# Fifteen-product matmul with tanh gating: four plain row tiles and twenty triples, w loaded by column pieces, seven x tiles transposed on TensorE, x sums on VectorE

## The chip, the core and the metric

The kernel runs on one core of one Trainium2 chip. The metric is the device time of one execution in microseconds. A core has five engines that run side by side and meet at semaphores: TensorE (PE in the profile, with PEld for its weight loads) multiplies and transposes, VectorE (DVE) and ScalarE (ACT) do elementwise work and can read PSUM, GpSimd (POOL) does elementwise work on SBUF and issues the DMA transfers that cast, and SyncE (SP) issues plain DMA transfers and DMA transposes. Each engine works through its own queue in order: an instruction that waits holds back everything queued behind it on that engine. PSUM, where matmul results land, has eight banks of 128 x 512 f32 here.

## The reference

x has 16 x 512 rows of 1024 numbers, w1 and w2 are 1024 x 768, all f32:

```python
y1 = np.matmul(x, w1)
y2 = np.matmul(x, w2)
return (np.tanh(y1) * y2).astype(np.float32)
```

## The kernel before

**Row tiles and pieces.** The rows of x are 64 tiles of 128. Multiplying wants x with its inner dimension across the partitions, so each tile is transposed into `xT`, eight blocks of 128 x 128 in f16. w1 and w2 stand side by side in f16 in `wh`. The 768 columns of each weight are cut into F = 512 and G = 256; the two G parts together are again 512 wide, so there are three column blocks ("a" of w1, "b" of w2, "M" for the two G parts), and with the inner dimension in two halves six weight blocks. A plain row tile needs 3 x 8 = 24 matmuls of 512 columns.

**Triples.** Three row tiles with six halves, times the six weight blocks, can be done with 15 products of sums of blocks instead of 18: `A_SUMS` lists ten sums of x halves for each triple (L385, `x_sum`), `B_SUMS` eleven sums of weight blocks made once (L375, `w_sum`), and `C_OPS` the 15 products p0 to p14 of four matmuls each (L426, `product`) with the additions (L441, `c_add`), copies and seeds (L432, `c_copy`), tanh (L444, `c_tanh`) and multiplies (L449, `c_mul`) that put them together in PSUM and SBUF. A triple costs 60 matmuls where three plain tiles cost 72. A number such as 32 or 24 names a block or a sum of blocks by its bits.

**What is plain.** The first `HEAD = 6` tiles and the last `TAIL = 1` are plain (L399 `mm`, L405 tanh, L409 multiply); 19 triples lie between. The last tile's three groups of matmuls are put into gaps near the end, behind the places `FILL = (-10, -6, -4)` of the product order.

**How x gets in.** Tiles 0 to 3 are loaded as f32 by SP (L307), transposed on TensorE into PSUM (L324) and copied to `xT` in f16 by VectorE or ScalarE. All other tiles are loaded by GpSimd with a cast to f16 into one of six `xh` buffers (L334) and transposed by a DMA that SP issues (L338) into `xT`, for which there are four buffers for each of three tags. GpSimd's first load stands behind a small copy, `gate`, that waits for the third slice of w2 (L470). The weights come as 16 slices of 128 x 768, four of them on ScalarE's queue (L311), and are cast to f16 by VectorE, ScalarE or, for w2, GpSimd (L317, L315).

**Side work.** ScalarE sums the absolute values of every x tile and weight slice (L341). At the end one flag says whether all of them were in a range where f16 serves; a general path stands behind a branch for the case that they weren't.

**What sets the order.** Everything is pinned in program order, and the order comes from `Planner`, a small list scheduler that runs when the kernel is built. Every step is an `op` with the engines that may run it and its cost there, a due time, what it needs, and what must have been issued or read before. It gives a step to an engine when it is ready, the earliest due first. The products' order on TensorE is fixed in `PE_ORDER`: the 15 products of a triple, where "+" marks those that are done one period later, among the next triple's. Five of the ten x sums are assigned to GpSimd by `ON_POOL`, the rest to VectorE:

```python
ON_POOL = (34, 35, 51, 10, 21)
...
op(f"S{v}.{i}", {"pool": 1.25} if v in ON_POOL else {"dve": 0.45}, ...)
```

Of the kernel before, what the change touches and what calls it, by code (L numbers as in the profile page):

```python
# [8 lines left out]
ACT = mybir.ActivationFunctionType  # L9
# [14 lines left out]

ON_POOL = (34, 35, 51, 10, 21)
# [48 lines left out]

PE_ORDER = "7 0+ 13+ 6 10 4+ 5+ 9 12 1 14 3+ 2+ 11 8"


class Planner:
# [3 lines left out]
    LATENCY = {"pe": 0.25, "act": 0.15, "dve": 0.15, "pool": 0.2, "sp": 1.6, "cast": 2.2}  # L82

    def __init__(self, n_banks):
        self.ops, self.strict, self.chains = {}, [], {}
        self.bank_free = [(0.0, b) for b in range(n_banks)]
        self.partial = set(range(n_banks))
        self.next = {}

    def op(self, name, engines, due, needs, fn, *args, behind=(), issued=(), chains=(), xfer=0.0, latency=None, seeds=False):  # L90


        assert name not in self.ops, name
        self.ops[name] = dict(engines=engines, due=due, needs=[n for n in needs if n], behind=[n for n in behind if n], issued=[n for n in issued if n], fn=fn, args=args,
                              chains=chains, xfer=xfer, latency=latency, seeds=seeds)
        for c in chains:
            self.chains.setdefault(c, {"left": 0, "bank": None, "end": 0.0})["left"] += 1

    def backward(self, margin):
# [4 lines left out]
        done, stack = {}, []  # L104
        for root in self.ops:
            stack.append((root, False))
            while stack:
# [9 lines left out]
                if "pe" not in o["engines"]:  # L117
                    cost = min(o["engines"].values()) + o["xfer"] + margin.get(n[0], 0.2)
                    due += [done[u] - cost for u in users[n]]
# [9 lines left out]
    def fitting(self, o):  # L129

        return [e for e in self.bank_free if not o["seeds"] or e[1] not in self.partial]

    def run(self):
        free = {"pe": 0.0, "act": 0.0, "dve": 0.0, "pool": 0.0, "sp": 0.0}
        bandwidth = 1.6
        left = {n: len(o["needs"] + o["behind"] + o["issued"]) for n, o in self.ops.items()}
        ready_at, end, engine_of, start_of = dict.fromkeys(self.ops, 0.0), {}, {}, {}
        ready = {e: [] for e in free}

        def release(n):  # L140
            for e in self.ops[n]["engines"]:
                ready[e].append(n)

        for n in self.ops:
            if not left[n]:
                release(n)
        position, lag = 0, 0.0
        strict = set(self.strict)
        while len(end) < len(self.ops):
            best = None  # L150
            for e, names in ready.items():
                options = []
                for n in names:
                    if n in strict and n != self.strict[position]:
                        continue
                    o = self.ops[n]
                    s = max(free[e], ready_at[n])
                    new = [c for c in o["chains"] if self.chains[c]["bank"] is None]
                    if new:
                        fit = self.fitting(o)  # L160
                        if not fit:
                            continue
                        s = max(s, min(fit)[0])
                    options.append((s, o["due"], n))
                if not options:
                    continue
                first = min(options)[0]
                s, due, n = min((o for o in options if o[0] <= first + 0.02), key=lambda o: o[1])
                urgent = [o for o in options if o[0] < first + 0.4 and o[1] + lag < min(due + lag, o[0] + 1.0)]
                if urgent and e != "pe":  # L170
                    s, due, n = min(urgent, key=lambda o: o[1])
                if best is None or s < best[0]:
                    best = s, e, n
            if not best:
                held = [c for c, v in self.chains.items() if v["bank"] is not None and v["left"]]
                print("held", [(c, self.chains[c]["left"], [n for n, o in self.ops.items() if c in o["chains"] and n not in end][:4]) for c in held], free)
            assert best, ("stuck", [(n, self.ops[n]["needs"]) for n in self.strict[position:position + 3]])
            s, e, n = best
            o = self.ops[n]
            for c in o["chains"]:  # L180
                if self.chains[c]["bank"] is None:
                    entry = min(self.fitting(o))
                    self.bank_free.remove(entry)
                    self.chains[c]["bank"] = entry[1]
                    if not o["seeds"]:
                        (self.partial.add if c[0] == "T" else self.partial.discard)(entry[1])
            f = s + o["engines"][e]
            free[e] = f
            if o["xfer"]:
                bandwidth = max(bandwidth, f) + o["xfer"]  # L190
                done = bandwidth + (o["latency"] or self.LATENCY["cast" if e == "pool" else "sp"])
            else:
                done = f
            end[n], engine_of[n], start_of[n] = done, e, s
            for k in o["engines"]:
                ready[k].remove(n)
            if n in strict:
                position += 1
                lag = s - o["due"]
            for c in o["chains"]:  # L200
                chain = self.chains[c]
                chain["end"] = max(chain["end"], done + self.LATENCY[e])
                chain["left"] -= 1
                if not chain["left"]:
                    self.bank_free.append((chain["end"], chain["bank"]))
            for u in self.next.get(n, ()):
                ready_at[u] = max(ready_at[u], f)
                left[u] -= 1
                if not left[u]:
                    release(u)  # L210
            for u in self.users[n]:
                same = e in ("act", "dve", "pe") and e in self.ops[u]["engines"]
                slack = 1.0 if n in self.ops[u]["behind"] and self.ops[u]["xfer"] else 0.0
                ready_at[u] = max(ready_at[u], done + slack + (0.05 if same else 0.0 if o["xfer"] else self.LATENCY[e]))
                left[u] -= 1
                if not left[u]:
                    release(u)
        self.end, self.engine_of, self.start_of = end, engine_of, start_of
        return sorted(self.ops, key=lambda n: start_of[n])
# [3 lines left out]
def kernel(  # L223
# [7 lines left out]

    nc = tc.nc
# [42 lines left out]
    ident = once.tile([P, P], f32, name="ident")  # L284
    wh = once.tile([P, KO, 2 * N], f16, name="wh")
# [4 lines left out]
    xfpool = head_stack.enter_context(tc.tile_pool(name="xf", bufs=4))  # L290
# [9 lines left out]

    xfs, wfs, xhs, xts, ss, cs, os_ = {}, {}, {}, {}, {}, {}, {}

    def load_xf(e, mt):
        xfs[mt] = xfpool.tile([P, K], f32, tag="xf", name="x_f")
        pin(nc.sync.dma_start(xfs[mt], xf[mt]))  # L307

    def load_w(e, t, k, queue):
        wfs[t, k] = wfpool.tile([P, N], f32, tag="wf", name="w_f")  # L310
        pin(queue.dma_start(wfs[t, k], wr[t][:, k, :]))  # L311
# [7 lines left out]
    def cast_w(e, t, k):  # L319
        copy(e, wh[:, k, t * N:(t + 1) * N], wfs[t, k])  # L320

    def transpose_pe(e, mt, h, chain):
        for k in range(KH):
            pin(nc.tensor.transpose(bank(chain)[:, k * P:(k + 1) * P],  # L324
                                    xfs[mt][:, (h * KH + k) * P:(h * KH + k + 1) * P], ident))

    def evacuate(e, mt, h, chain):
        if h == 0:
            xts[mt] = xtpool.tile([P, KO, P], f16, tag=f"xT{mt % 3}", name="xT")
        copy(e, xts[mt][:, h * KH:(h + 1) * KH, :].rearrange("p k m -> p (k m)"), bank(chain))  # L330

    def load_x(e, mt):
        xhs[mt] = xhpool.tile([P, K], f16, tag="xh", name="xh")
        pin(nc.gpsimd.dma_start(xhs[mt], xf[mt]))  # L334
# [9 lines left out]
    def abs_x(e, mt):  # L344
        abs_sum(e, (xfs if mt in xfs else xhs)[mt], mt)
# [433 lines left out]
```

## Time and profile before

| what | value |
|---|---|
| runs, us | 315.31, 893.4, 320.95 |
| median, us | 320.95 |
| span of the profiled execution, us | 312.9 |
| mean granted TensorE clock in it | 0.988 |
| PE / DVE / ACT / POOL busy, share of the span | 95% / 77% / 70% / 47% |
| HBM read / written, MB | 39.85 / 25.17 |

The profiled execution has no time of its own among the runs; its span, from the first to the last instruction, is 312.9 us, and the shortest run took 2.4 us more than that. One of the three runs stands far apart from the others, so the median is the longer of the two ordinary ones.

A row of a group of instructions has its line, engine, operation, the tiles it writes and reads, the shape, how often it ran; then busy time, the mean duration of one in ns, and how long the engine was idle ahead of them, and for whom. A row of the timeline has the start and the length in us, engine, line and operation, and in brackets the idle time ahead of it and who ended it. A matmul's duration includes its way through the array, so that neighbours overlap; what it costs is the distance between starts.

### The profile page before, as it was taken

The numbers are of one execution on the slowest core, as the hardware profiler recorded it, in microseconds if no ns is written. First come the engines' busy times: TensorE is split into PE (matmuls) and PEld (weight loads), VectorE is DVE, ScalarE is ACT, GpSimd is POOL, SyncE is SP. The second block draws the span as 40 slices with busy tenths as digits, with TensorE's granted clock in tenths as the row PEclk, the third lists the DMA queues.
The fourth block names the chain that finished last, engine by engine and source line by source line (L and its number), as shares of the span: only waits on it lengthen the run. The fifth ranks groups of instructions, "written<-read, shape, count | busy, mean of one in ns | idle before, by whom it ended". The sixth has DMA issues, their size and how long they took to land.

```text
span 312.9 us, 4544 instructions
## 1 busy us (share of the span) xinstructions
PE 296.1 (95%) x1394; PEld 137.9 (44%) x1394; DVE 239.9 (77%) x406; ACT 218.0 (70%) x430; POOL 146.6 (47%) x163
## 2 busy tenths in 40 slices
PE   8999596999998999989999999999999999999993
PEld 5665242444443444434444444444444444444441
DVE  0549669988879888788887878878788888887643
ACT  4987565697987999586776868768677685544641
POOL 0033257665647773726646466473655644440000
PEclk9999798899999999999999999999999999999999
DMA  7999999999999999999999999999999999112033
GB/s 287 407 389 180 159 176 169 257 209 196 279 224 255 287 242 237 170 206 213 190 210 161 289 211 169 249 188 225 226 178 226 204 210 265 76 77 112 38 153 154
DMA packets 84122, 65.33 MB, mean 209 GB/s; under 512 B 65664, under 2 KB 65664, under 8 KB 84096
## 3 DMA queue, kind: packets, MB, share of 16 engines
q1 hardware_dynamic: 74880, 47.72, 64.4%
q0 software_dynamic: 8640, 15.73, 32.4%
q10 hardware_dynamic: 576, 1.57, 1.3%
q8 instruction: 11, 0.18, 0.3%
q14 instruction: 15, 0.12, 0.1%
HBM read 39.85 MB, written 25.17 MB: 208 GB/s over the span
## 4 chain that ended last, share of the span: by engine, by line
PE 47%; DMA 6%; issue 3%; POOL 1%; ACT 1%; DVE 1%; SPq 1%; POOLq 0%; ACTq 0%
PE bank L426 45%; DMA xh<-in_x_dram 4%; DMA out_dram<-o 2%; PE bank L399 2%; POOL s L385 1%; SPq L338 1%; DVE s L385 0%; ACT o L444 0%; ACT bank L432 0%; DVE bank L441 0%; DVE o_last L409 0%; ACT junk L341 0%; SPq L393 0%; ACT s L432 0%; PE bank L464 0%
## 5 line engine op out<-in xcount | busy, mean ns | idle before, releaser
L426 PE MATMUL bank<-b,s 128*128 128x512 f16 x608 | 142.5, 382 | 3.3 <-DVE bank L441 3.3
L426 PEld LDWEIGHTS <-s 128*128 128x128 f16 x760 | 74.7, 98 | 96.5 <-issue 8.5
L441 DVE TENSOR_TENSOR bank<-bank,s 128x512 f32<-128x512 f32 x95 | 65.8, 693 | 19.6 <-PE bank L426 10.5
L432 ACT ACTIVATE s<-bank 128x512 f32<-128x512 f32 x95 | 56.2, 594 | 32.1 <-PE bank L426 31.2
L385 POOL TENSOR_TENSOR s<-xT 128x512 f16<-128x512 f16 x38 | 44.7, 1177 | 58.5 <-PE bank L426 52.4
L341 ACT ACTIVATE junk<-xh 128x1024 f16<-128x1024 f16 x60 | 63.2, 1054 | 8.0 <-DMA xh<-in_x_dram 7.4
L449 DVE TENSOR_TENSOR o<-o,bank 128x256 f32<-128x256 f32 (+1 forms) x114 | 59.1, 546 | 7.5 <-ACT o L444 6.1
L426 PEld LDWEIGHTS <-xT 128*128 128x128 f16 x380 | 37.0, 98 | 47.0 <-issue 2.9
L426 PE MATMUL bank<-b,xT 128*128 128x512 f16 x228 | 55.4, 379 | 0.0
L444 ACT ACTIVATE o<-bank 128x256 f32<-128x256 f32 x76 | 33.0, 436 | 25.2 <-DVE bank L441 17.2
L399 PE MATMUL bank<-wh,xT 128*128 128x512 f16 (+1 forms) x200 | 39.8, 355 | 4.2 <-DMA xT<-xh 3.6
L334 POOL DMA_DIRECT2D xh<-in_x_dram x60 | 34.3, 572 | 13.9 <-DMA xT<-xh 10.0
L426 PE MATMUL bank<-wh,xT 128*128 128x512 f16 x152 | 39.0, 379 | 1.6 <-ACT o L444 1.6
L426 PE MATMUL bank<-wh,s 128*128 128x512 f16 x152 | 39.0, 379 | 1.3 <-ACT bank L432 1.3
L385 POOL TENSOR_TENSOR s<-s,s 128x512 f16<-128x512 f16 x19 | 22.9, 1208 | 36.7 <-DVE s L385 36.7
L385 DVE TENSOR_TENSOR s<-s,xT 128x512 f16<-128x512 f16 x57 | 35.0, 613 | 4.5 <-PE bank L426 4.3
L399 PEld LDWEIGHTS <-xT 128*128 128x128 f16 x200 | 19.7, 100 | 22.8 <-DMA xT<-xh 3.9
L444 ACT ACTIVATE o<-s 128x512 f32<-128x512 f32 x38 | 23.7, 624 | 3.5 <-DVE s L441 3.5
L385 POOL TENSOR_TENSOR s<-xT,s 128x512 f16<-128x512 f16 x19 | 22.6, 1189 | 4.3 <-PE bank L426 4.3
L432 ACT ACTIVATE bank<-bank 128x512 f32<-128x512 f32 x38 | 20.7, 573 | 4.9 <-PE bank L426 3.9
L385 POOL TENSOR_TENSOR s<-s,xT 128x512 f16<-128x512 f16 x19 | 22.4, 1179 | 0.6
L385 DVE TENSOR_TENSOR s<-xT 128x512 f16<-128x512 f16 x19 | 17.7, 931 | 4.6 <-PE bank L426 3.2
(41 smaller groups left out, 144.5 us busy)
## 6 DMA issues: line engine op xcount, KB each, us to landing
out_dram<-o SPq DMA_DIRECT2D x63, 384.0 KB, 6.3
xh<-in_x_dram POOLq DMA_DIRECT2D x60, 256.0 KB, 7.0
w_f<-in_w_dram SPq DMA_DIRECT2D x12, 384.0 KB, 8.2
x_f<-in_x_dram SPq DMA_DIRECT2D x4, 512.0 KB, 7.0
w_f<-in_w_dram ACTq DMA_DIRECT2D x4, 384.0 KB, 7.6
xT<-xh SPq DMA_TRANSPOSE x60, 6.2
out_dram<-o_last SPq DMA_DIRECT2D x1, 384.0 KB, 3.3
```

Of the source, the lines that this page charges most:

```text
L334: pin(nc.gpsimd.dma_start(xhs[mt], xf[mt]))
L338: pin(nc.sync.dma_start_transpose(xts[mt], xhs[mt]))
L341: pin(nc.scalar.activation(junk[:, :src.shape[-1]], src, ACT.Abs, scale=scale, accum_out=sums[:, column:column + 1]))
L385: pin(engine[e].tensor_tensor(ss[i, v], x_operand(i, a), x_operand(i, b), OP[how]))
L399: pin(nc.tensor.matmul(b, xts[mt][:, k, :], rhs, start=first, stop=k == KO - 1, skip_group_check=True))
L426: pin(nc.tensor.matmul(place(i, dst), x_operand(i, a)[:, k, :], w_rhs(b, k), start=begins and k == 0, stop=k == KH - 1, skip_group_check=T ...
L432: pin(nc.scalar.activation(d, place(i, src), ACT.Copy, scale=float(sign)))
L441: pin(nc.vector.tensor_tensor(d, a, b, ALU.add if signs == (1, 1) else ALU.subtract))
L444: pin(nc.scalar.activation(out_tile(HEAD + 3 * i + r)[:, lo:lo + n], place(i, src)[:, :n], ACT.Tanh, scale=float(sign)))
L449: pin(nc.vector.tensor_tensor(o, o, place(i, src)[:, at:at + n], ALU.mult))
```

## The change

It does these things at once:

- `HEAD` is 4 and there is no plain tail: 20 triples.
- A weight is loaded in pieces of 256 KB: "a" and "b" pieces are the first 512 columns of one slice of w1 or w2, "g" and "h" pieces are the last 256 columns of two slices. All 24 go through SP, together with the two halves of x tile 1, in a written order, `SP_LOADS`. There are 12 staging buffers for them where there were 8 larger ones. In `wh` the two G parts now lie next to each other, so that every weight block is one contiguous run of 512 columns.
- Tiles 0, 2, 3 (plain) and 4, 5, 6 (the first triple) are loaded by GpSimd with a cast, in the order of `POOL_LOADS`; an entry such as `2.0:a3` is a half tile with a gate that waits for piece a3. They are transposed in f16 on TensorE, and tile 1 in f32. From tile 7 on a DMA transposes. `XH_BUFS` is 4 where it was 6.
- Of triple 0, nine products are put in an order of their own, `PE_FIRST`, among the plain matmuls.
- All ten x sums of a triple run on VectorE.
- The "b" part of plain tile 3 (eight matmuls of 512 columns) is held back to the end as two sets of eight 256-column matmuls, `HELD`, behind the fifth last and the last product.
- Casts of w no longer run on GpSimd; copies of C run on ScalarE alone, as they did in effect.
- The planner is rewritten: it moves in time, has an occupancy and a latency for each step, three DMA parameters for each transfer with queues that share the bandwidth, and chooses by due time among what can start now or a little later. The order that it gives may differ everywhere.
- 13 matmuls on a constant ahead of the work, where there were 21.

The core of the diff:

```diff
-ON_POOL = (34, 35, 51, 10, 21)
...
 PE_ORDER = "7 0+ 13+ 6 10 4+ 5+ 9 12 1 14 3+ 2+ 11 8"
+PE_FIRST = "10 7 1 6 12 9 11 8 14"
...
+SP_LOADS = "h4 h6 a6 a1 a4 a5 h2 x1.1 b6 b7 g6 b1 x1.0 g2 h0 b2 g4 b4 g0 b5 a2 a3 a0 a7 b3 b0"
+POOL_LOADS = "2.1 0 2.0:a3 6:g0 4 5 3.1:b3 3.0:b4"
...
-    HEAD = 6
-    TAIL = 1
-    TRIPLES = (MT - HEAD - TAIL) // 3
+    HEAD = 4
+    TRIPLES = (MT - HEAD) // 3
...
-    XH_BUFS, XT_BUFS, S_BUFS, O_BUFS, C_BUFS, WF_BUFS = 6, 4, 2, 4, 2, 8
-    WARM = 21
-    AHEAD = 3
-    GATE = 2
-    FILL = (-10, -6, -4)
+    XH_BUFS, XT_BUFS, S_BUFS, O_BUFS, C_BUFS, WF_BUFS = 4, 4, 2, 4, 2, 12
...
+    FIRST = 2, 1
+    WARM = 13
...
+    def load_w(e, c, k):
+
+        wfs[c, k] = wfpool.tile([P, F], f32, tag="wf", name="w_f")
+        if c in "ab":
+            pin(nc.sync.dma_start(wfs[c, k], wr["ab".index(c)][:, k, :F]))
+        else:
+            pin(nc.sync.dma_start(wfs[c, k].rearrange("p (k n) -> p k n", k=2), wr["gh".index(c)][:, k:k + 2, F:]))
...
+    COLUMNS = {"a": 0, "g": F, "h": N, "b": 2 * F}
...
+    def transpose_16(e, mt, lo, n, chain):
+        b = bank(chain).bitcast(f16)
+        for k in range(lo, lo + n):
+            pin(nc.tensor.transpose(b[:, (k - lo) * P:(k - lo + 1) * P], xhs[mt][:, k * P:(k + 1) * P], ident_h))
...
+    def evacuate_16(e, mt, lo, n, chain):
+        copy(e, xt_tile(mt)[:, lo:lo + n, :].rearrange("p k m -> p (k m)"), bank(chain).bitcast(f16)[:, :n * P])
...
-            op(f"S{v}.{i}", {"pool": 1.25} if v in ON_POOL else {"dve": 0.45}, None, x_needs(i, a) + x_needs(i, b), x_sum, i, v, a, b, how,
+            op(f"S{v}.{i}", {"dve": DVE_S}, None, x_needs(i, a) + x_needs(i, b), x_sum, i, v, a, b, how,
...
+    HELD = {0: -5, 1: -1}
+    for h, at in HELD.items():
+        chain = ("held", h)
+        last = []
+        for n, k in enumerate(K_ORDER):
+            name = f"m3b{k}{h}"
+            op(name, {"pe": (MM / 2, MM / 2)}, 1e4, [f"cb{k}", part(HEAD - 1, k)], mm, chain, HEAD - 1, k, 2 * F, h * G, G,
+               behind=[plan.strict[at]], chains=[chain])
+            last.append(name)
+        op(f"mu3b{h}", {"dve": DVE_G}, 1e4, last + ["th3a"], plain_mul, HEAD - 1, h * G, G, chain, h * G, chains=[chain])
...
+            op(f"L{mt}", {"pool": (0.55, 0.55)}, None, [], load_x, mt, 0, KO, issued=[pool_last],
+               behind=[f"D{old}"] + on_pe.get(old, [f"T{old}"]) if old else [], dma=("pool", 1.38, 1.84, 0.6, 0.172))
...
+            op(f"T{mt}", {"sp": (1.25, 1.25)}, None, [f"L{mt}"], transpose, mt, issued=[sp_last],
+               behind=xt_readers[mt - 3 * XT_BUFS] if mt >= 3 * XT_BUFS and mt - 3 * XT_BUFS != HEAD - 1 else [], dma=("sp", 1.15, 1.84, 0.6, 0.018))
```

More of the change, by code (lines that the diff above doesn't have):

```diff
@@ new lines, in run @@
+        ops, engines = self.ops, ("pe", "act", "dve", "pool", "sp")
+        free = dict.fromkeys(engines, 0.0)
+        left = {n: len(o["needs"]) + len(o["behind"]) + len(o["issued"]) for n, o in ops.items()}
+        ready_at = dict.fromkeys(ops, 0.0)
+        self.start_of, self.end, self.engine_of = {}, {}, {}
+        ready = {e: [] for e in engines}
+        strict = {n: z for z, n in enumerate(self.strict)}
+        position, lag = 0, 0.0
+        queues, moved, heap, known, done = {}, 0.0, [0], {0}, {}
@@ L201, in run @@
+        for n in ops:
+            if not left[n]:
+                for e in ops[n]["engines"]:
+                    ready[e].append(n)
+        while heap:
+            tick = heapq.heappop(heap)
+            known.discard(tick)
+            t = tick / 1e4
+            for c in done.pop(tick, ()):
                 chain = self.chains[c]
-                chain["end"] = max(chain["end"], done + self.LATENCY[e])
                 chain["left"] -= 1
                 if not chain["left"]:
-                    self.bank_free.append((chain["end"], chain["bank"]))
@@ L206, in run @@
[L206 to L217, printed above, removed]
@@ L222 @@
+        if len(self.start_of) < len(ops):
+            missing = [n for n in ops if n not in self.start_of]
+            raise RuntimeError(f"stuck: {[n for n in missing if not left[n]][:20]} {missing[:12]} {position} {self.strict[position:position + 3]} "
+                               f"{[(c, v) for c, v in self.chains.items() if v['bank'] is not None and v['left']][:10]}")
+        return sorted(ops, key=lambda n: self.start_of[n])
 @with_exitstack
@@ new lines, in casts, with w_needs, x_needs @@
+    def casts(v):
+        bit = v.bit_length() - 1
+        ks = range(bit // 3 * KH, (bit // 3 + 1) * KH)
+        return [f"c{c}{k}" for c in ("a", "b", "gh")[bit % 3] for k in ks if c in "ab" or k % 2 == 0]
+    def w_needs(v):
+        return [f"B{v}"] if v in wsum else casts(v)
+    for v, a, b, how in B_SUMS:
+        op(f"B{v}", {"dve": DVE_B}, None, w_needs(a) + w_needs(b), w_sum, v, a, b, how)
+    def x_needs(i, v):
+        if v & (v - 1):
+            return [f"S{v}.{i}"]
+        bit = v.bit_length() - 1
+        return [part(HEAD + 3 * i + bit // 2, bit % 2 * KH)]
```

572 lines of the change are left out of this document (305 added, 267 removed).

## The prediction

> **What bounds the kernel now.** I read the page first, then busy time by stretches, then the timeline of TensorE in the first 75 us, then the chain of waits at the end, and last the groups of VectorE and GpSimd.
>
> ```profile
> span 312.9 us, 4544 instructions
> PE 296.1 (95%) x1394; PEld 137.9 (44%) x1394; DVE 239.9 (77%) x406; ACT 218.0 (70%) x430; POOL 146.6 (47%) x163
> ```
> ```profile
> 35.00:40.00 5.00, 4.99 (x16) 1.98 (x17) 1.25 (x4) 0.60 (x1) 1.59 (x3) 0.66 1.07 165
> 50.00:60.00 10.00, 7.21 (x26) 2.98 (x26) 10.00 (x12) 4.83 (x10) 6.71 (x8) 0.83 1.20 199
> 65.00:300.00 235.00, 231.70 (x1070) 104.33 (x1069) 190.69 (x338) 171.02 (x341) 122.70 (x129) 1.00 0.99 202
> 140.00:160.00 20.00, 20.00 (x95) 9.04 (x93) 16.21 (x30) 14.02 (x29) 13.17 (x15) 1.00 1.07 211
> ```
> ```profile
> 5.34 1.04 PE L324 MATMUL bank<-ident,x_f 128*128 128x128 f32 x8
> 6.62 0.50 PE L399 MATMUL bank<-wh,xT 128*128 128x512 f16 x2 [0.24 <-ACT xT L315]
> ...
> 13.37 18.04 PE L399 MATMUL bank<-wh,xT 128*128 128x512 f16 x110
> 35.01 1.52 PE L399 MATMUL bank<-wh,xT 128*128 128x512 f16 x5 [3.60 <-DMA xT<-xh]
> ```
> ```profile
> 52.79 4.44 PE L426 MATMUL bank<-b,s 128*128 128x512 f16 x12 [2.98 <-DVE bank L441]
> ...
> 63.97 4.48 PE L426 MATMUL bank<-b,s 128*128 128x512 f16 x20
> 68.29 1.03 PE L426 MATMUL bank<-wh,s 128*128 128x512 f16 x4
> ```
> ```profile
> 305.67 2.17 PE bank L399 x10
> ...
> 307.87 0.69 DVE o_last L409
> ```
>
> The numbers of a stretch are its length, then busy time of PE, weight load, DVE, ACT and POOL, the granted clock, DMA share and GB/s. TensorE is the bound: between 65 and 300 us it is busy 231.70 of 235, and in 140 to 160 all of it. Twenty matmuls take 63.97 to 68.29, so one costs 4.32/20 = 0.216 us. The kernel issues 1140 product matmuls and the equal of 168 full plain ones: 1308 x 0.216 = 282.5 us. The other 30.4 of 312.9 us is what can be won: 6.6 until the first plain matmul; 24.8 from there to 31.4 (13.37 + 18.04) for four plain tiles that need 96 x 0.216 = 20.7, so 4.1; 3.6 of idle until 35.0, waiting for the first tile that a DMA transposes; 1.7 for the clock of 0.66 over the next 5 us; 3.0 of idle before 52.8 and 1.7 for the clock of 0.83 around it; 3.3 between 65 and 300; 5.1 from the last matmul (305.67 + 2.17) to the end. About 1.3 are scattered. The start carries more than half of it, and the start is what the change rewrites.
>
> **Fewer matmuls.** Four plain tiles and twenty triples are 4 x 24 + 20 x 60 = 1296 matmuls, 12 fewer: 279.9 us, a gain of 2.6 on the bounding engine.
>
> **The x sums leave GpSimd.**
>
> ```profile
> L385 POOL TENSOR_TENSOR s<-xT 128x512 f16<-128x512 f16 x38 | 44.7, 1177 | 58.5 <-PE bank L426 52.4 <-DMA xT<-xh 6.1
> L385 DVE TENSOR_TENSOR s<-s,xT 128x512 f16<-128x512 f16 x57 | 35.0, 613 | 4.5 <-PE bank L426 4.3
> L385 DVE TENSOR_TENSOR s<-xT 128x512 f16<-128x512 f16 x19 | 17.7, 931 | 4.6 <-PE bank L426 3.2 <-DMA xT<-xh 1.4
> L385 DVE TENSOR_TENSOR s<-xT,s 128x512 f16<-128x512 f16 x19 | 8.0, 422 | 1.3
> ```
> ```profile
> 47.77 0.41 DVE L385 TENSOR_TENSOR s<-xT,s 128x512 f16<-128x512 f16 x1
> 48.11 0.41 DVE L409 TENSOR_TENSOR o<-o,bank 128x256 f32<-128x256 f32 x1
> 48.44 1.26 DVE L385 TENSOR_TENSOR s<-s,xT 128x512 f16<-128x512 f16 x1
> ...
> 52.05 0.69 DVE L441 TENSOR_TENSOR bank<-bank,s 128x512 f32<-128x512 f32 x1
> 52.65 0.67 DVE L441 TENSOR_TENSOR s<-s,bank 128x512 f32<-128x512 f32 x1
> ```
>
> The same f16 sum takes 0.41 us on VectorE at one place and 1.26 at another; groups of one shape average 422, 613 and 931 ns. GpSimd is adding f16 tiles in the same stretches, and without its sums I take 0.42 for all. Then VectorE's ten sums of a triple end sooner than today's five beside five of 1.18 on GpSimd. Starts lie closer than durations: 0.34 for the sum (47.77 to 48.11), 0.33 for a 256-column multiply, 0.60 for a 512-column f32 operation (52.05 to 52.65). A triple has 8 f32 additions, 3 wide and 3 narrow multiplies and now 10 sums: 11 x 0.60 + 3 x 0.33 + 10 x 0.34 = 11.0 us in the 60 x 0.216 = 12.96 that TensorE needs. Today it is busy 16.21/20 x 12.96 = 10.5. It stays under the bound, so I cost this at nothing; the cover is the 1.96 us of slack per triple, and what it costs without that is the second rival. GpSimd's load issues lose the sums that they queue behind.
>
> **The start.** The order of w and x pieces matters only as far as bytes arrive.
>
> ```profile
> 0.00:5.00 5.00, 3.93 (x19) 2.82 (x20) 0.17 (x1) 1.28 (x1) 0.70 (x6) 1.00 0.64 218
> 5.00:10.00 5.00, 4.16 (x30) 2.81 (x29) 1.85 (x3) 3.89 (x7) 0.00 (x0) 1.00 1.02 412
> 10.00:15.00 5.00, 5.00 (x36) 3.31 (x35) 2.41 (x4) 4.53 (x9) 0.00 (x0) 1.00 1.03 402
> 15.00:20.00 5.00, 5.00 (x34) 3.05 (x32) 2.24 (x4) 3.89 (x9) 0.00 (x0) 1.00 1.03 399
> ```
> ```profile
> q0 software_dynamic: 8640, 15.73, 32.4%
> ```
> ```profile
> xh<-in_x_dram POOLq DMA_DIRECT2D x60, 256.0 KB, 7.0
> xT<-xh SPq DMA_TRANSPOSE x60, 6.2
> out_dram<-o_last SPq DMA_DIRECT2D x1, 384.0 KB, 3.3
> ```
> ```profile
> 26.48 21.65 SPq L338 DMA_TRANSPOSE xT<-xh  x8
> ```
>
> By the rates, 1.09 MB have come by 5 us, 3.15 by 10, 5.16 by 15. GpSimd's second half of tile 2 waits for piece a3, the 22nd of SP's 26 pieces of 0.262 MB: 5.77 MB, and 0.79 read for tile 0 and the half of tile 2 ahead of it, are there at 15 + (6.55 - 5.16)/0.40 = 18.5 us. From issue to landing a casting load takes 7.0 in the median; a lone store took 3.3. SP's stream is over by then, so I take 5.0: 23.6. Until then only tiles 0, 1 and half of 2 can be multiplied, 60 matmuls, 13.0 us, and 20 transposes, from about 7.0 (6.6 now; the first weights used are SP's third piece). That fits in 16.6 us, so TensorE waits some there and is load-bound until 23.6.
>
> Further casting loads follow at between 0.524 MB/0.402 = 1.3 us each and 0.324 x 312.9/60 = 1.7, the time their packets take among other traffic; I take 1.5. Tile 6 is there at 25.1, 4 at 26.6, 5 at 28.1, 3 at 29.6, while TensorE has 28 plain matmuls, 36 of triple 0, and 36 transposes left. Eight f32 transposes took 1.04 us with the last lasting 0.27, so 0.11 each; f16 ones can't be seen, and the floor is 128/512 of 0.216, 0.054. I take 0.11, the row of the same operation and shape. So 64 x 0.216 + 36 x 0.11 = 17.8, with 0.7 for the first evacuation: triple 1 begins at 42.1 (39.9 by the floor).
>
> It begins with a product on tile 9, by the DMA path: GpSimd's queue carries 7, 8 and 9 behind tile 3, landing at 31.1, 32.6, 34.1 (four xh buffers: 8 and 9 also wait for tiles 6 and 4 to be transposed and summed). A transpose lands 6.2 after its issue, tile 9 at 40.3; where SP needs 21.65/8 = 2.7 per transpose, at 42.7. I count no wait, though 0.6 is possible and more if a load slips; this is the thin place, and the first rival.
>
> The rest of the start lies beside this. The eleven sums of weight blocks stay on VectorE:
>
> ```profile
> L375 DVE TENSOR_TENSOR b<-wh 128x2048 f16<-128x2048 f16 x6 | 8.5, 1440 | 0.0
> ```
>
> Even at 1.44 us each they are 15.8 of the 35 between 7 and 42; ScalarE shares casts and evacuations with it, and loses four w loads of its own queue to SP. On SP the head's stores come behind the transposes of tiles 13 and later, so nothing waits for them but their own buffers. Three DMA transposes fewer cost nothing where TensorE is busy anyway.
>
> **Rest and end.** From triple 1 there remain 1296 - 64 - 60 = 1172 matmuls, 253.2 us: 295.3. I keep the 3.3 us lost between 65 and 300, between nothing and twice that. The end has eight half-wide pairs of tile 3 to fill gaps where the old end had 24 matmuls; the last sums between p5, p3 and p2 (an addition of 0.69 and a copy of about 0.6) leave about 1.0 open, between 0 and 2. Then 5.1 as now. Span: 295.3 + 3.3 + 1.0 + 5.1 = 304.7, against 312.9. The two ordinary runs took 315.31 and 320.95, so 2.4 us lie around the span in the shorter, and the median shown, 320.95, is 5.6 above that. On the shorter's footing: **307.1 us**.
>
> **A rule weighed.** The idle time of 3.6 us was followed by a clock of 0.66, that of 2.98 by twelve matmuls in 4.44, (4.44 - 0.38)/11 = 0.37 each instead of 0.216. The Trainium skill, TensorE: Matmul & The Clock Gate, section "What's actually happening", halves the clock after an idle window of about 3.4 us, counted in free-running windows. The second stall shows that a shorter gap suffices here; by the rule read strictly the next rival would be 1.7 cheaper.
>
> **Rivals.** *Tiles 9 to 12 come late* (0.20). For it: the loads' 7.0 and transposes' 6.2 in the median, tile 9's margin of -0.6 to 1.8, four xh buffers for six, and a first stall of this kind in the trace. Against: nothing on GpSimd delays the issues any more. If both early stalls come back with their clock, 3.6 + 1.7 + 3.0 + 1.7 = 10.0, less the scattered bits already counted: 311 to 317, no clear change.
>
> *VectorE becomes the bound*, the slower case (0.10). It waits in order ahead of its additions:
>
> ```profile
> L441 DVE TENSOR_TENSOR bank<-bank,s 128x512 f32<-128x512 f32 x95 | 65.8, 693 | 19.6 <-PE bank L426 10.5 <-ACT o L444 4.3 <-ACT s L432 3.9
> L441 DVE TENSOR_TENSOR s<-bank,s 128x512 f32<-128x512 f32 x19 | 13.0, 685 | 7.9 <-ACT s L432 7.9
> ```
>
> That is 27.5/19 = 1.4 us per triple; 11.0 + 1.4 = 12.4 is still below 12.96, but if the sums stand alone in the queue and each costs its whole duration, it is 8 x 0.69 + 3 x 0.69 + 3 x 0.41 + 10 x 0.42 = 13.0, with waits 14.4: 1.4 x 20 = 29 us more, 336. It decides from 0.7 us per triple over the bound, where 307 passes 321. Against it: PE never starved in 140 to 160 with VectorE at 16.21 of 20.
>
> *TensorE paces the start too* (0.20): no load is waited for from 7.0 on. Then 7.0 + 124 x 0.216 + 0.9 + 48 x 0.054 = 37.3 at triple 1, no loss at the end: 37.3 + 253.2 + 3.3 + 5.1 + 2.4 = 301, and 298 if the steady losses vanish. Against it: the a3 gate, by the bytes.
>
> *Transposes run cold* (0.03). The f32 row's single matmul lasts 274 ns though eight overlap; if f16 ones don't overlap, 36 x (0.27 - 0.11) = 6 more: 313. The Trainium skill, TensorE: Matmul & The Clock Gate, section "PE-mode transpose", gives about 275 ns in a kernel and says that they don't hold the clock up; the trace's duration agrees, its spacing does not.
>
> **The numbers.** The forecast, 302 to 311, has 0.47. The range goes from 298 to 318: it leaves out the VectorE case and the ends of the others, some 0.17. About 2% is what a measurement of this kernel can tell from no change: the two runs lie 1.8% apart. Two percent below the shorter run is 309, below the median 314.5. Faster: 0.20 of the paced start, most of the forecast (0.40), and a share of the late and cold cases on the upper footing (0.08): 0.68. Slower: the VectorE case and a remainder, 0.11. Within: 0.21.
>
> **What would show it.** First product of triple 1 near 42; no wait for xT over 2 us there (the late rival shows 3 us and a clock under 0.8 behind it); all VectorE sums near 420 ns and none on GpSimd; DVE at 16 to 18 of 20 in the middle with PE at 20 (the VectorE rival: PE under 18.5); f16 transposes at 0.05 to 0.11 apart. I am wrong if TensorE starves in the steady part, where I count 3.3 us, or if the start is not bound by bytes.

## The result and the profile after

| | before | after |
|---|---|---|
| median, us | 318.99 (4 runs) | 334.19 (4 runs: 334.50, 333.88, 332.52, 337.75) |
| ratio to before | 1 | 1.059, 95% interval 1.047 to 1.071 |
| span of the profiled execution, us | 312.9 | 332.6 |

The change made the kernel 6% slower; I had forecast 307, with 0.11 for slower. A ratio here and below compares the shorter runs of each kernel alone, without those over 1.5% above its shortest, while a median is over all its runs, which is why 1.059 is not 334.19/318.99. The page of the changed kernel, first two lines of engine time:

```profile
span 332.6 us, 4501 instructions
PE 297.2 (89%) x1374; PEld 134.6 (40%) x1374; DVE 253.6 (76%) x513; ACT 227.2 (68%) x455; POOL 38.0 (11%) x76
```

Every engine is busy for a smaller share of the span than before, so that no engine looks like a new bound: someone waits for someone. Busy time by stretches of the changed kernel (length, then busy us and count on PE, weight load, DVE, ACT and POOL, granted clock, DMA share, GB/s):

```profile
10.00:15.00 5.00, 4.64 (x19) 2.33 (x17) 1.12 (x2) 2.90 (x6) 0.00 (x0) 0.51 1.07 380
50.00:60.00 10.00, 6.79 (x26) 2.70 (x24) 5.43 (x13) 5.64 (x12) 1.59 (x3) 0.80 1.11 185
65.00:300.00 235.00, 219.65 (x1001) 97.94 (x1000) 196.55 (x410) 168.65 (x344) 23.85 (x45) 0.99 0.93 195
140.00:160.00 20.00, 15.75 (x67) 6.63 (x65) 12.52 (x26) 10.40 (x22) 2.12 (x4) 0.91 1.05 195
```

Between 65 and 300 us TensorE is idle for 15.4 us (235 less 219.65), where it was 3.3, and 140 to 160, full before, lacks 4.3. Who waits, longest in total first (us, times, longest):

```profile
POOL xh L423 <- ACT junk L429: 98.0, 23, 10.5
POOL xh L423 <- DMA xT<-xh: 65.9, 18, 7.9
ACT s L497 <- PE bank L493: 39.7, 36, 3.5
ACT junk L429 <- DMA xh<-in_x_dram: 34.7, 25, 4.3
...
PE bank L493 <- ACT bank L497: 11.8, 12, 3.2
...
PE bank L493 <- ACT s L497: 6.3, 4, 4.2
```

ScalarE's sum of absolute values (`abs_x`, "junk") now waits 34.7 us for its casting load, 25 times. In the kernel before it was 8 times:

```profile
ACT junk L341 <- DMA xh<-in_x_dram: 7.4, 8, 3.6
```

TensorE's waits are on ScalarE's copies of partial results, and GpSimd's loads wait for the sums. The chain that ended last in the changed kernel has that loop in a row (start, length, what):

```profile
105.23 6.10 DMA xh<-in_x_dram
111.37 0.04 issue
111.41 0.27 ACT junk L429
111.69 0.69 issue
112.38 0.20 ACT junk L429
112.57 0.27 issue
112.84 7.32 DMA xh<-in_x_dram
120.19 0.04 issue
120.23 1.15 ACT junk L429 x2
121.38 0.27 ACT o L507
121.65 0.50 ACT s L497
122.19 14.47 PE bank L493 x67
```

A load lands, its sum runs, that frees a buffer for the next load, that one lands, its sum runs, and only then the tanh and the copy that stand behind the sum on ScalarE, and then TensorE. ScalarE's timeline at TensorE's first long wait behind the start, then TensorE's there, and then both engines at the longest wait:

```profile
51.21 0.62 ACT L507 ACTIVATE o<-s 128x512 f32<-128x512 f32 x1
55.22 1.06 ACT L429 ACTIVATE junk<-xh 128x1024 f16<-128x1024 f16 x1 [3.40 <-DMA xh<-in_x_dram]
56.18 0.19 ACT L429 ACTIVATION_READ_ACCUMULATOR junk<-xh 128x1 f32 x1
56.28 1.06 ACT L497 ACTIVATE bank<-bank 128x512 f32<-128x512 f32 x2
```
```profile
56.91 1.86 PE L493 MATMUL bank<-wh,s 128*128 128x512 f16 x4 [3.21 <-ACT bank L497]
```
```profile
153.08 1.06 ACT L429 ACTIVATE junk<-xh 128x1024 f16<-128x1024 f16 x1 [4.32 <-DMA xh<-in_x_dram]
154.04 0.19 ACT L429 ACTIVATION_READ_ACCUMULATOR junk<-xh 128x1 f32 x1
154.13 0.58 ACT L507 ACTIVATE o<-bank 128x512 f32<-128x512 f32 x1
154.61 0.59 ACT L497 ACTIVATE s<-bank 128x512 f32<-128x512 f32 x1
```
```profile
155.25 1.87 PE L493 MATMUL bank<-wh,xT 128*128 128x512 f16 x4 [4.18 <-ACT s L497]
156.91 3.45 PE L493 MATMUL bank<-b,s 128*128 128x512 f16 x12
```

In the longest case ScalarE stands for 4.32 us until 153.08, while TensorE has been done since 151.07 (155.25 less 4.18): the tanh and the copy behind the sum could have run two microseconds earlier. In the first case ScalarE stands for 3.40 us until 55.22, TensorE runs dry for 3.21 from 53.70, and the clock of 0.80 in 50 to 60 follows. It is the rule and not two cases: of the 17 gaps over 0.25 us that TensorE has behind 44 us, 15 begin during such a wait of ScalarE or within 2.5 us behind it, and they make 17.9 of 19.4 us.

**Theory A**, then: the plan places a tile's absolute sum on ScalarE soon after the time at which it believes the casting load has landed. The plan has 0.55 + 1.84 + 1.38 + 0.6 = 4.4 us for that load, and 1.84 + 1.15 + 0.6 = 3.6 for a transpose, or more where transfers share the bandwidth; the profile has 5.9 and 5.7 in the median. With four buffers, a load waits for the transpose and the sum of the tile four before it, so the two errors add. ScalarE stands, and TensorE after it. **Theory B**: VectorE, with ten sums in its in-order queue, is the bound in disguise. **Theory C**: four buffers and the DMA's latency bring the transposed tiles too late, whatever ScalarE does.

### The profile page after: what moved, and what is told of

The parts are those of the page before. It is cut to its first block, busy times and chain, and to the rows that moved or that the text cites. A ratio compares the mean times of both kernels' runs of the same rounds, so it can differ in the third digit from the quotient of the medians.

```text
span 332.6 us, 4501 instructions
## 1 busy us (share of the span) xinstructions
PE 297.2 (89%) x1374; PEld 134.6 (40%) x1374; DVE 253.6 (76%) x513; ACT 227.2 (68%) x455; POOL 38.0 (11%) x76
## 4 chain that ended last, share of the span: by engine, by line
DMA 38%; PE 34%; issue 12%; ACT 10%; DVE 2%; POOL 2%; ACTq 0%; DVEq 0%; POOLq 0%; SPq 0%
PE bank L493 32%; DMA xh<-in_x_dram 30%; DMA xT<-xh 7%; ACT junk L429 6%; ACT bank L497 2%; ACT o L507 2%; PE bank L471 1%; ACT s L497 1%; DVE bank L504 1%; POOL xh L423 1%; DVE o L511 1%; POOL held L530 1%; PE bank L415 0%; DVE o_last L478 0%; POOL ident masks.py:199 0%
## 5 line engine op out<-in xcount | busy, mean ns | idle before, releaser
L493 PE MATMUL bank<-b,s 128*128 128x512 f16 x640 | 149.2, 381 | 0.0
L429 ACT ACTIVATE junk<-xh 128x1024 f16<-128x1024 f16 x63 | 66.6, 1057 | 35.0 <-DMA xh<-in_x_dram 34.7
L504 DVE TENSOR_TENSOR bank<-bank,s 128x512 f32<-128x512 f32 x100 | 69.6, 696 | 24.6 <-ACT o L507 15.5
L511 DVE TENSOR_TENSOR o<-o,bank 128x512 f32<-128x512 f32 (+1 forms) x120 | 62.9, 547 | 21.8 <-ACT o L507 20.6
L493 PEld LDWEIGHTS <-xT 128*128 128x128 f16 x400 | 39.5, 99 | 59.1 <-issue 14.2
L493 PE MATMUL bank<-wh,s 128*128 128x512 f16 x160 | 41.9, 385 | 10.6 <-ACT bank L497 10.6
L493 PE MATMUL bank<-wh,xT 128*128 128x512 f16 x160 | 41.9, 385 | 6.6 <-ACT s L497 5.1
L457 DVE TENSOR_TENSOR s<-xT 128x512 f16<-128x512 f16 x60 | 24.8, 416 | 0.9 <-PE bank L493 0.8
L471 PE MATMUL bank<-wh,xT 128*128 128x512 f16 x72 | 18.4, 404 | 0.8 <-ACT xT L387 0.5
L457 DVE TENSOR_TENSOR s<-xT,s 128x512 f16<-128x512 f16 x40 | 16.8, 419 | 0.5
L504 DVE TENSOR_TENSOR bank<-s,bank 128x512 f32<-128x512 f32 x20 | 13.8, 692 | 3.8 <-PE bank L493 1.9
L504 DVE TENSOR_TENSOR s<-s,bank 128x512 f32<-128x512 f32 x20 | 13.6, 679 | 0.6 <-issue 0.6
L429 ACT ACTIVATE junk<-wh 128x768 f16<-128x768 f16 x16 | 13.5, 846 | 0.1
L504 DVE TENSOR_TENSOR s<-bank,s 128x512 f32<-128x512 f32 x20 | 13.6, 680 | 0.0
```

Source lines behind the costliest of these rows:

```text
L429: pin(nc.scalar.activation(junk[:, :src.shape[-1]], src, ACT.Abs, scale=scale, accum_out=sums[:, column:column + 1]))
L457: pin(engine[e].tensor_tensor(ss[i, v], x_operand(i, a), x_operand(i, b), OP[how]))
L471: pin(nc.tensor.matmul(bank(chain)[:, lo:lo + n], xts[mt][:, k, :], wh[:, k, c + lo:c + lo + n], start=begun[chain] == 1, stop=begun[chain ...
L493: pin(nc.tensor.matmul(place(i, dst), x_operand(i, a)[:, k, :], w_block(b)[:, k, :], start=begins and k == 0, stop=k == KH - 1, skip_group ...
L504: pin(nc.vector.tensor_tensor(d, a, b, ALU.add if signs == (1, 1) else ALU.subtract))
L511: pin(nc.vector.tensor_tensor(o, o, place(i, src)[:, at:at + n], ALU.mult))
```

## The experiments

Each ran beside the kernel before on the same chip, and a ratio is to that kernel; runs 1 to 4, 5 to 8, 9 to 11 and 12 were on four different chips.

**1. Without the absolute sums of x tiles 7 to 63**, all else in the same order. Their results are set beforehand:

```diff
     def abs_x(e, mt):
-        abs_sum(e, x32[mt] if mt in x32 else xhs[mt], mt)
+        if mt in parts:
+            abs_sum(e, x32[mt] if mt in x32 else xhs[mt], mt)
...
+    pin(nc.vector.memset(sums, 800.0))
```

> The changed kernel with every instruction in the same order, but without ScalarE's absolute sums of x tiles 7 to 63 (their 57 columns are set to 800 beforehand, so the range check of x sees only tiles 0 to 6). Theory A (ScalarE stands in its queue before a sum whose casting load has not landed, TensorE then waits for ScalarE's copies, and the next load waits for the sum): ScalarE's wait for xh, 34.7 us, goes, GpSimd's wait for the sums, 98 us, goes; TensorE's losses between 65 and 300 us fall from 15.4 to under 4: span 312 to 318 (from 332.6). Theory B (VectorE's ten sums in its in-order queue are the bound): the span falls by less than 4 us, since VectorE's work is as before. Theory C (four xh buffers and DMA latency hold the transposed tiles back): less than half of the loss goes.

Median 313.85 us (310.27 to 317.08), ratio 0.968 (0.962 to 0.974), span 309.8, a little below A's range of 312 to 318:

```profile
65.00:300.00 235.00, 230.72 (x1072) 104.67 (x1071) 204.96 (x427) 129.14 (x261) 23.75 (x45) 1.00 1.04 204
```

TensorE and VectorE had the same instructions in the same order, so B falls. TensorE lost time behind late tiles once, 3.5 us near 90. C does not fall with this run alone, since a load no longer waits for a sum either, and ScalarE has 40 us less to do in this stretch; run 2 keeps both.

**2. The sum planned after the transpose.** The sum reads the same tile and computes the same, at a later place. The planner runs anew, so other instructions move too: VectorE's and ScalarE's by some places, TensorE's hardly.

```diff
-        op(f"D{mt}", {"act": ACT_D}, ORIGIN - 10 + 4.33 * (mt - HEAD), loads_of(mt), abs_x, mt)
+        op(f"D{mt}", {"act": ACT_D}, ORIGIN - 10 + 4.33 * (mt - HEAD), [f"T{mt}"] if mt not in parts else loads_of(mt), abs_x, mt)
```

> One planner line: the absolute sum of a tile is planned when its DMA transpose has landed rather than when its load has; it computes the same and reads the same tile. Theory A: ScalarE's wait for xh falls from 34.7 to under 6 us; the span to 314 to 320, a little above the run without sums, as the four xh buffers come free a little later. Theory B: 330 or more. Theory C: the span stays or grows, as buffers are held longer.

310.94 us (310.31 to 311.77), ratio 0.968 (0.964 to 0.972), span 310.0: below my expectation's range, and as fast as without the sums. This one line turns 6% slower into 3% faster; I call it the mended kernel. The 3% is beside a kernel before that took 319.93 to 322.99 us on that chip; its medians on the other three were 317.12 to 319.36 and its shortest run 313.94, so that the gain elsewhere may be between 1 and 2.5%. Its stretches and ScalarE's group of sums (busy us, mean ns, idle before):

```profile
65.00:300.00 235.00, 231.16 (x1073) 104.66 (x1071) 205.67 (x423) 177.13 (x349) 23.24 (x44) 1.00 0.96 200
140.00:160.00 20.00, 20.00 (x94) 9.07 (x93) 17.98 (x37) 15.14 (x29) 2.64 (x5) 1.00 1.20 209
```
```profile
L429 ACT ACTIVATE junk<-xh 128x1024 f16<-128x1024 f16 x63 | 66.5, 1055 | 4.6 <-DMA xh<-in_x_dram 3.8
```

ScalarE's wait for loads is 3.8 us where it was 34.7, and TensorE is full in the middle with VectorE at 17.98 of 20. The four buffers are still there, and GpSimd's loads still wait 61.1 us for the sums: that wait alone need not cost anything, and C falls. Run 1 shows what the sums cost where they stood, with nothing else moved; run 2 shows that they can stay.

**3. Six xh buffers in memory**, the order unchanged:

```diff
-    xhpool = pool("xh", XH_BUFS)
+    xhpool = pool("xh", 6)
```

> Six xh buffers instead of four, the order of all instructions unchanged (the planner still plans for four). Theory A: loads are issued two tiles earlier, so that the sums find their tile landed: ScalarE's wait for xh falls to under 10 us and the span to 314 to 322. Theory B: 330 or more. Theory C (buffers are the cause, ScalarE's place in the order is not): the same gain as A here, but none in the run that plans the sum later.

Median 324.45 (318.51 to 326.17); the profile is of the shortest, with a span of 316.7, inside A's range, and the other three, 322.4 to 324.4, are just above it. ScalarE waited 8.2 us. From 100 to 280 us TensorE was busy for all 180, but it lost 6.5 us between 70 and 100. Earlier loads spare ScalarE, as A has it, and cost something else, which shows in run 9.

**4. Longer latencies in the plan:**

```diff
-               behind=[...] if old else [], dma=("pool", 1.38, 1.84, 0.6, 0.172))
+               behind=[...] if old else [], dma=("pool", 1.38, 1.84, 2.8, 0.172))
...
-               behind=[...], dma=("sp", 1.15, 1.84, 0.6, 0.018))
+               behind=[...], dma=("sp", 1.15, 1.84, 2.8, 0.018))
```

> The planner is told that casting loads and DMA transposes land 2.8 us after their last byte instead of 0.6 (the profile shows 5.9 and 5.7 us from issue to landing, the plan has 4.4 and 3.6). Four buffers stay. Theory A: the sums move later, ScalarE's wait for xh falls to under 12 us, span 314 to 322. Theory B: 330 or more. If the waits come from spread rather than from the plan's mean, it helps by less than half: 324 to 330.

Median 328.25, ratio 1.023 (1.018 to 1.029). ScalarE still waited 29.6 us, 17 times. Correcting the plan's mean gave back 5.9 us of span, of the 22.6 that run 2 gave. That fits a sum which is planned right at the expected landing and so is exposed to every load that comes later than expected; it takes slack, as in run 2. It is one plan's evidence, since this edit also moves everything else that waits for a load or a transpose.

**5. The kernel before with all sums on VectorE:**

```diff
-ON_POOL = (34, 35, 51, 10, 21)
+ON_POOL = ()
```

> The kernel before, with one part of the change alone: all ten x sums of a triple on VectorE. Theory A (the sums' move is harmless or good, the loss came from ScalarE's sums of absolute values): sums at about 420 ns instead of 613 and 931, the idle time near 50 us gets shorter, time 0.97 to 1.00 of before. Theory B (VectorE in order is the bound): 1.02 or more, with TensorE waiting for VectorE in every triple.

319.91, ratio 1.007 (1.002 to 1.013): inside neither theory's range. The sums did fall to one duration, and ScalarE's wait for loads rose from 7.4 to 12.8 us:

```profile
L385 DVE TENSOR_TENSOR s<-s,xT 128x512 f16<-128x512 f16 x76 | 31.5, 416 | 0.0
L385 DVE TENSOR_TENSOR s<-xT 128x512 f16<-128x512 f16 x57 | 23.6, 415 | 7.3 <-DMA xT<-xh 7.3
```

The move alone neither pays nor costs much in the old order, although in the profile TensorE lost 7.9 us between 65 and 300 where it had lost 3.3.

**6. The kernel before with its absolute sums planned after the transpose:**

```diff
-       op(f"D{mt}", {"act": 1.25}, ORIGIN - 12 + 4.33 * (mt - HEAD), [f"L{mt}"], abs_x, mt)
+       op(f"D{mt}", {"act": 1.25}, ORIGIN - 12 + 4.33 * (mt - HEAD), [f"T{mt}"], abs_x, mt)
```

> The kernel before, with its absolute sums planned after the DMA transpose, as in the mended kernel. Theory A: its ScalarE waited for xh only 7.4 us in all, of which TensorE felt about 2, so the time is 0.985 to 1.00 of before. If a good part of the mended kernel's gain came from something else in the new place of the sums, this is below 0.98.

Median 320.2 (312.02 to 323.41) beside 319.36: no difference that this spread can show. ScalarE's wait for loads is gone from its list. The profile is of a run of 322.73, and in it a stall near 50 us is longer than before (TensorE 2.14 of 10 in 50 to 60); whether the 312.02 had it too is not known. A gain like the mended kernel's does not show.

**7. The mended kernel with five sums back on GpSimd:**

```diff
-            op(f"S{v}.{i}", {"dve": DVE_S}, None, ...
+            op(f"S{v}.{i}", {"pool": (1.18, 1.2)} if v in (34, 35, 51, 10, 21) else {"dve": DVE_S}, None, ...
```

> The changed kernel with the sums planned after the transpose (310.9 us), and the five x sums that GpSimd had given back to it. Theory A: VectorE's f16 sums slow to 600 ns and more beside GpSimd, GpSimd's loads queue behind its sums, 312 to 322. If VectorE's load were what costs, 304 to 309.

326.48, ratio 1.024 (1.013 to 1.035), 15.5 us slower than the mended kernel and beyond my range. Two thirds of that is lost before triple 1, which begins at 55.4 us, where the mended kernel's begins at 44.8; most of it is one stall (timeline of that run):

```profile
41.21 2.17 DVE L447 TENSOR_TENSOR b<-b,b 128x2048 f16<-128x2048 f16 x1
42.27 2.13 POOL L457 TENSOR_TENSOR s<-xT,s 128x512 f16<-128x512 f16 x1
...
45.89 2.59 DVE L447 TENSOR_TENSOR b<-b,wh 128x2048 f16<-128x2048 f16 x1
...
49.13 1.44 PE L493 MATMUL bank<-b,s 128*128 128x512 f16 x3 [7.62 <-DVE s L504]
```

The last two weight sums, 1.21 each in the mended kernel, take 2.17 and 2.59 beside GpSimd's, and two x sums between them 1.37 and 1.36 instead of 0.42: 4.2 of the 7.62 us. The rest of the stall may come from the new order. So the sums' move helps the new start, where VectorE has the weight sums to do at the same time; that it is needed there is likely but not shown, since this plan differs as a whole. What is lost behind the start, 4.7 us, I did not take apart.

**8. The mended kernel with six xh buffers, planned for six:**

```diff
-    XH_BUFS, XT_BUFS, S_BUFS, O_BUFS, C_BUFS, WF_BUFS = 4, 4, 2, 4, 2, 12
+    XH_BUFS, XT_BUFS, S_BUFS, O_BUFS, C_BUFS, WF_BUFS = 6, 4, 2, 4, 2, 12
```

> The changed kernel with the sums planned after the transpose, and six xh buffers, for which the planner plans too. Theory A: what the mended kernel still loses between 70 and 105 us (about 3.5 us, on late tiles after the start) shrinks: 306 to 311. If four buffers are enough once ScalarE does not block, no change: 310 to 312.

337.0 (329.59 to 337.96): a miss, with the longest median of all. The profile is of the longest run. In it ScalarE is not to blame (3.6 us). Waits and DMA issues (us to landing):

```profile
DVE s L457 <- DMA xT<-xh: 35.1, 10, 6.5
PE bank L493 <- DVE bank L504: 18.4, 6, 5.4
```
```profile
xh<-in_x_dram POOLq DMA_DIRECT2D x61, 256.0 KB, 8.4
...
xT<-xh SPq DMA_TRANSPOSE x57, 10.6
```

VectorE's x sums now stand ahead of tiles that have not been transposed, 35.1 us in all, TensorE waits 18.4 us for VectorE, and a transpose lands after 10.6 us where the mended kernel has 6.4. It looks like theory A's mechanism on another engine; no run takes that wait away to show it.

**9. The mended kernel's own order, six buffers in memory:** the edit of run 3 on the mended kernel.

> The mended kernel (sums planned after the transpose) with six xh buffers in memory, its order unchanged, planned for four. If more loads in flight are what hurt in the run that also planned for six (337 us), this is slower than 310.9 too, 315 or more. If it was that plan's order, in which VectorE's x sums stand ahead of tiles that have not been transposed (it waited 35 us for them), this is 306 to 311.

320.74 (319.21 to 322.69), ratio 1.013 (0.999 to 1.027), span 317.5 against 310.0. Not one instruction stands elsewhere than in the mended kernel, and yet VectorE's wait for transposes rises from 6.9 to 16.2 us. Their time to landing between 30 and 65 us, in the mended kernel and then in this run, and what followed from one that was issued at 56.7 and landed 13.8 us later:

```profile
DMA to landing us min/median/max: 3.1/5.3/7.7
```
```profile
DMA to landing us min/median/max: 4.2/8.2/14.2
```
```profile
70.55 0.43 DVE L457 TENSOR_TENSOR s<-xT 128x512 f16<-128x512 f16 x1 [5.12 <-DMA xT<-xh]
...
72.25 3.39 PE L493 MATMUL bank<-b,xT 128*128 128x512 f16 x8 [3.13 <-ACT bank L497]
```

VectorE stands for it, and TensorE behind it, through a copy of ScalarE's that waits for VectorE. With two more loads in flight the early transposes land later. Runs 2 and 9 have the same order, and so have the changed kernel and run 3, where the slowest early transpose goes from 7.9 to 12.5 us. The median over the whole run would not tell this: it is 7.3 here, but 7.1 in run 1 and 7.0 in run 11, which have four buffers and spans under 310. It explains why run 3 gained less than A alone would give, and probably a part of run 8.

**10. The mended kernel, planned with the latencies of run 4.**

> The mended kernel, planned with casting loads and transposes landing 2.8 us after their last byte instead of 0.6. If optimistic landing times in the plan are the general cause, VectorE's wait for xT falls from 6.9 us, the losses between 70 and 105 us go: 305 to 310. If the plan with long latencies is worse for other reasons (alone it gave 328), 315 or more.

Median 316.99 (311.86 to 328.53 in ten runs), ratio 0.988 (0.982 to 0.993): no better than the mended kernel, whose longest run was 311.77, and a miss for the first case. In the profile, of a run of 318.04, VectorE waited 10.0 us for transposes, not less than 6.9. Longer latencies in the plan did not make a better order, and I can't say why.

**11. The mended kernel with 30 constant matmuls at the start** (`WARM = 30`).

> The mended kernel with 30 constant matmuls ahead of the work instead of 13, so that TensorE has no 2.4 and 3.3 us gaps before 10 us. If the slow clock of the start (0.51 between 10 and 15 us in the changed kernel's profile) costs on the path, 1 to 3 us less than 310.9: 308 to 310. If the start is bound by bytes, no change: 310 to 312.

Median 312.4 (309.3 to 316.25), span 308.1 in the profile: no change that can be told. The first plain matmul stays near 10.2 us. The clock in 10 to 15 us was 0.67 in its profile and 1.00 in the mended kernel's without the extra matmuls, so that the run did not test what I had meant. It shows another thing: ScalarE waited 17.3 us for loads here, with TensorE busy 232.43 of 235 between 65 and 300. ScalarE's wait is not a price by itself; it costs where what is queued behind it is due.

**12. The kernel before with the two things that A blames:**

```diff
-    LATENCY = {"pe": 0.25, "act": 0.15, "dve": 0.15, "pool": 0.2, "sp": 1.6, "cast": 2.2}
+    LATENCY = {"pe": 0.25, "act": 0.15, "dve": 0.15, "pool": 0.2, "sp": 1.6, "cast": 0.6}
...
-    XH_BUFS, XT_BUFS, S_BUFS, O_BUFS, C_BUFS, WF_BUFS = 6, 4, 2, 4, 2, 8
+    XH_BUFS, XT_BUFS, S_BUFS, O_BUFS, C_BUFS, WF_BUFS = 4, 4, 2, 4, 2, 8
...
-           ..., xfer=1.2, latency=3.0)
+           ..., xfer=1.2, latency=1.0)
```

> The kernel before, given the two things that theory A blames: four xh buffers (six before), and a plan in which casting loads land 0.6 us after their last byte (2.2 before) and transposes 1.0 (3.0 before). Everything else as before, five x sums on GpSimd too. Theory A: ScalarE's wait for xh rises from 7.4 us to 20 or more, and the time to 1.02 to 1.06 of before. If it needs something else of the change as well (sums on VectorE, the new planner), the time stays within 1.02.

330.78, ratio 1.045 (1.037 to 1.053). Its waits and the steady stretch:

```profile
ACT junk L341 <- DMA xh<-in_x_dram: 40.1, 22, 4.3
```
```profile
65.00:300.00 235.00, 223.25 (x1019) 98.63 (x1018) 188.59 (x326) 161.75 (x329) 123.55 (x130) 1.00 0.93 199
```

The old kernel, old planner, sums on GpSimd and all, becomes nearly as slow as the changed one when loads and transposes are expected early and there are four buffers; ScalarE waits 40.1 us. Not all of that loss goes through ScalarE: 7.9 of the 18.0 us of TensorE's gaps over 0.25 us behind 44 us follow such a wait, and the longest gap, 4.58 us before 54.8, waits for VectorE. Which of the two things does more was not tried.

## Why the prediction was wrong

**The failed step** is "I keep the 3.3 us lost between 65 and 300, between nothing and twice that". It measured 15.4. Over the whole stretch from triple 1 to the last matmul, 1172 matmuls, I had 253.2 + 3.3 + 1.0 = 257.5 us, and it took 280.4 (44.9 to 325.3): 19.7 us of idle time, and 7.5 around it, of which 4.3 are the extra time of 21 matmuls that run 0.427 apart instead of 0.216 behind the two longest gaps. That is 22.9 of the 27.9 us by which the span missed; the start has 2.8 of them and the end 2.2. I took this loss over as a constant of the steady part, though the change altered both things that set it: the buffers that a load waits for, and the plan's idea of when it lands. The sentence that hid it is the first rival's "nothing on GpSimd delays the issues any more": GpSimd then waited 98.0 us for ScalarE's sums, and ScalarE for GpSimd's loads. I had named four buffers and the transposed-and-summed condition, but only for tiles 8 and 9, and never followed what is queued behind a sum on ScalarE.

Both the loss and its cause are shown: taking the sums out with nothing else moved (run 1), and planning them later (run 2), give back 20 to 23 us, each alone. That early landings and four buffers bring it about is shown in part: they make the old kernel 4.5% slower (run 12), but there ScalarE's waits account for less than half of TensorE's gaps.

**The other terms.**
- *Matmul price and count*: 1172 matmuls after the start at 0.216. In the mended kernel the 124th matmul begins at 44.6 us and the last at 302.9: 258.3, against 257.5 forecast. With ScalarE out of the way this part is right to 1 us.
- *The start*: I had the 124 matmuls done at 42.1 (42.0 without a slip: 18.5 + 5.0 is 23.5); in the changed kernel they are at 44.9. The first plain matmul came at 10.5, not 7.0: tile 0's casting load, issued at 2.8, landed only 6.9 us later, at a DMA share of 1.05 in 5 to 10 us. The clock of 0.51 in 10 to 15 us follows TensorE's idle time ahead of it, and does not show in the start: with a clock of 1.00 there, triple 1 begins at 44.8 in the mended kernel and at 46.5 in run 3, which has the changed kernel's order. The f16 transposes took the floor: sixteen in 1.06 us, 0.055 apart, where I had taken 0.11; the eight at 9.70, at the low clock, are 0.107 apart. The start was no faster than the old one: the old kernel had begun its 124th matmul, counted in 512 columns, at 42.5.

```profile
9.70 1.03 PE L415 MATMUL bank<-ident_h,xh 128*128 128x128 f16 x8 [3.24 <-DMA xh<-in_x_dram]
10.53 0.63 PE L471 MATMUL bank<-wh,xT 128*128 128x512 f16 x1
...
30.00 1.06 PE L415 MATMUL bank<-ident_h,xh 128*128 128x128 f16 x16
```

- *The sums on VectorE*: costed at nothing, and right in the steady part: all at 416 to 421 ns, TensorE full beside VectorE at 17.98 of 20 in the mended kernel. What they seem to save at the start (run 7) I had not seen.
- *The end*: 7.3 us from the last matmul where I had 5.1; the last two stores are issued at 326.2 and 326.7 beside each other and land at 331.2 and 331.5.
- *The rivals*: VectorE as the bound fell with runs 1 and 2. Tile 9 was transposed by 42.2 and nobody waited for it on TensorE; a stall of the size that the late rival names did come, 3.21 us before 56.9, but behind ScalarE's copy. The cold transposes fell by their spacing. None of the rivals was the case: the slower one that I named blamed the engine that got more work, and the one that failed was an engine whose work had hardly changed (ScalarE, 218.0 us busy before and 227.2 after).

With the mended order the change is faster, as I had forecast: 310.9 against 307, 3.2% under the kernel before on its chip and less beside the same kernel's times on others. With run 11, its variant, it is the fastest version run here.

## What to carry to other kernels

In an order written out ahead, side work that reads a DMA's result must stand on its engine well after the time at which the DMA is believed to land: place it where the work itself already waits for something later (here the transpose), not where the engine looks idle. When a buffer count or a latency in the plan changes, look for the engine that waits for that DMA, what is queued behind it, and what its end releases. And more buffers are not safer by themselves: here, loads that ran further ahead came with later landings of the transposes that were needed first.

## What the hardware showed that I had not expected

Two more casting loads in flight, with every instruction in the same place, cost 7.5 us of span (317.5 against 310.0); the transposes issued between 30 and 65 us rose from 5.3 to 8.2 us in the median and from 7.7 to 14.2 at most. f16 transposes on TensorE ran 0.055 us apart while the f32 ones of the kernel before lie 0.11 apart. And the length of a gap did not settle what the clock did behind it: behind 2.25 us (run 4, before 246.4) 512-column matmuls ran 0.427 us apart, behind 3.53 us (run 1, before 91.5) 0.215.
